# Recurrent mixer of a three-layer kernel: the products of w issued first at a scan, one scaled copy taken into a product, and a scale spread by transposes

## The chip, the cores and the metric

The kernel runs on one core of one Trainium2 chip. The metric is the device time of one execution in microseconds (us), from the first to the last instruction and a little around them; lower is better. The engines of a core are named as the profile names them: PE (TensorE's matmuls) and PEld (its weight loads), DVE (VectorE), ACT (ScalarE), POOL (GpSimd) and SP (SyncE, which issues most of the DMAs).

## What is computed

The whole kernel is a hybrid layer with three mixers and an MLP, an attention layer with an MLP, and a recurrent layer (RWKV-7) with an MLP, on 512 positions of width 1024, in 32-bit floats. The change lies in the recurrent mixer alone. Of its reference this matters:

```python
kk = heads(k * k_k)
kk = kk / jnp.maximum(jnp.sqrt(jnp.sum(kk * kk, axis=-1, keepdims=True)), 1e-12)
for d in range(2):
    ...
    decay = jnp.exp(-jnp.exp(w_log.astype(F32)))
    a = jax.nn.sigmoid(a0[d] + (xa @ a1[d]) @ a2[d])
    ...
    o = rwkv7_scan(*ins)

def step(state, inp):
    r_t, w_t, k_t, v_t, kk_t, a_t = inp
    sa = jnp.einsum('bhvk,bhk->bhv', state, -kk_t)
    state = (state * w_t[:, :, None, :] + sa[..., None] * (kk_t * a_t)[:, :, None, :]
             + v_t[..., None] * k_t[:, :, None, :])
    return state, jnp.einsum('bhvk,bhk->bhv', state, r_t)
```

There are 16 heads of 64, and two directions d; in the second the sequence runs backwards.

## The kernel before

The recurrence is not stepped through. `rwkv` puts two heads on the 128 partitions (a pair p, 0 to 7) and treats a pair in one direction as a stream q = 2p + d, 0 to 15. The 512 positions of a stream are 8 chunks of 64. Within a chunk everything is matrix products; from chunk to chunk a 64x64 state per head goes on. A stream passes three stages, written as generators, and a pair one more:

- `pair(p)` (L1278 to L1298): the keys of a pair are normalised. The squares are summed per head on PE (L1169), POOL takes the power -1/2 (L1172), DVE spreads the result over a 128x512 tile (L1176), and PE turns that tile over with four matmuls against the identity (L1179); DVE multiplies the keys by it (kk, L1292) and ACT makes a half of them (kkh, L1294).
- `prep(q)`: decays, gates and the scores. L1309 is the matmul of the decays and gates, L1311 to L1325 their functions on ACT, L1317 DVE's running sum along the positions, L1326 the product that reads kkh, L1335 and L1336 the products with the decays (ar and bk), L1350 the scores on PE and L1353 their masks on DVE. Two of the masked tiles (sc) go to DRAM through eight DMAs (lu, L1360).
- `invert(q)`: POOL inverts the 16x16 diagonal blocks of the scores (L1418, L1420, thirty small instructions), SP stores them (xu, L1427) and loads them in another layout (X, L1431); then DVE turns X over (L1439), and PE, DVE and ACT complete the inverse (L1446 to L1479).
- `scan(q)`: L1494 makes w and vs of all chunks on PE, taken to SBUF by ACT (L1495, L1497). Then products of all chunks: kb with vs (L1504, DVE scales it to n, L1505), w with kb (L1509, DVE adds the identity to make m, L1510), w with the scores (L1515, DVE adds it to ar, L1516), and the scores with vs (L1523, into the output's PSUM tile). Then the chain over the chunks: six times a PE product of m and n (L1528) and a DVE step (L1529) that makes the next n; PE adds each chunk's output (L1533). A norm and a gate follow (L1538 to L1565).

The loop at the end of `rwkv` steps a clock t; every 16 steps a new stream enters each stage, so that in one period a scan, the prep and the inversion of the next streams, and the big "fill" products (fil: L1214, L1230, L1247, 128x512 each) are interleaved on every engine. All instructions of an engine run in the order in which they were put in its queue; a scheduler sets that order from the order of the code, the yields and priorities. An instruction at the head of a queue that waits for another engine holds back all that stands behind it. A 32-bit matmul of the program is two MATMUL instructions in the trace; a transpose is one.

Of the kernel before, what the change touches and what calls it, by code (L numbers as in the profile page):

```python
# [8 lines left out]
F32 = mybir.dt.float32  # L9
F32R = mybir.dt.float32r  # L10
AF = mybir.ActivationFunctionType
ALU = mybir.AluOpType
# [5 lines left out]
S = 512  # L18
# [991 lines left out]
class L3:  # L1010
# [120 lines left out]
    def rwkv(self, lp, rkd, xr, vm, tw, ta, sg):  # L1131
        nc, tc, I = self.nc, self.tc, self.I
        with ExitStack() as cx:
            pool = lambda n, b, **kw: cx.enter_context(tc.tile_pool(name=n, bufs=b, **kw))
            arp, vsp, bkp, unp, sp, wk = (pool(n, b) for n, b in (
                ("ar", 4), ("vs", 3), ("bk", 1), ("un", 2), ("s3", 2), ("wk", 2)))
# [9 lines left out]
            eye = lp.tile([128, 64], F32, name="eye")  # L1146
# [12 lines left out]
            def c8(x):  # L1159
                return x.rearrange("p (c t) -> p c t", c=8)  # L1160

            def flip(x, d):
                return x[:, ::-1] if d else x

            def head_scale(sq, fn):

                ps = self.psm.tile([128, S], F32, tag="mm", name="mm")
                for b in range(4):
                    nc.tensor.matmul(ps[:, 2 * b:2 * b + 2], sq[:, b * 128:(b + 1) * 128], bones, start=True, stop=True)  # L1169
                c = sp.tile([128, 8], F32, tag="hs", name="hs", bufs=4)  # L1170
                fn(c, ps[:, 0:8])
                nc.gpsimd.tensor_tensor(c, c, self.mhalf, op=ALU.pow)  # L1172
                for _ in range(7):
                    yield
                e = T().rearrange("p (b h t) -> p b h t", b=4, h=2)
                nc.vector.tensor_copy(e, c.rearrange("p (b h) -> p b h", h=2).unsqueeze(3).to_broadcast([128, 4, 2, 64]))  # L1176
                ps = self.psm.tile([128, S], F32, tag="mm", name="mm")
                for b in range(4):
                    nc.tensor.matmul(ps[:, b * 128:(b + 1) * 128], e[:, b].rearrange("p h t -> p (h t)"), self.ident,  # L1179
                                     start=True, stop=True)  # L1180
                return ps

            turn = [0]
# [11 lines left out]
            def mm():  # L1195
                return self.psm.tile([128, 8, 64], F32, tag="mm", name="mm")

            H = [(h, slice(64 * h, 64 * h + 64), slice(64 - 64 * h, 128 - 64 * h)) for h in range(2)]
# [79 lines left out]
            def pair(p):  # L1278

                r[p], k[p] = (self.xnp.tile([128, S], F32, tag="xl", name=n) for n in "rk")  # L1280
                nc.sync.dma_start(k[p], rkd[p, 1])
                nc.sync.dma_start(r[p], rkd[p, 0])
                for _ in range(8):
                    yield
                wst = lora2(p, 0, 2)
                kkr, sq = T(), T()
                nc.scalar.activation(kkr, k[p], AF.Copy, scale=self.vec("k_k", p))
                nc.scalar.activation(sq, kkr, AF.Square)
                yield
                ps = yield from head_scale(sq, lambda c, ps: nc.vector.tensor_scalar_max(c, ps, 1e-24))  # L1290
                kk = wk.tile([128, S], F32, tag="kk", name="kk", bufs=1)
                nc.vector.tensor_tensor(kk, kkr, ps, op=ALU.mult)  # L1292
                kkh = wk.tile([128, S], F32, tag="kkh", name="kkh", bufs=1)
                nc.scalar.activation(kkh, kk, AF.Copy, scale=0.5)  # L1294
                rkw = wk.tile([128, 128], F32, tag="rkw", name="rkw")
                nc.vector.tensor_scalar_mul(rkw, bfull, self.vec("r_k", p))
                P[p] = wst, kk, kkh, rkw
                yield  # L1298

            def prep(q, C):  # L1300

                p, d = divmod(q, 2)
                wst, kk, kkh, rkw = P[p]

                ps, pa = (self.psm.tile([128, S], F32, tag="mm", name="mm") for _ in range(2))
                for i, (a, b) in enumerate(((0, 0), (0, 1), (1, 0))):
# [3 lines left out]
                s = T()  # L1310
# [12 lines left out]
                nc.scalar.copy(dl, dp[:, :, 64])  # L1323
                kd = T()
                nc.scalar.activation(kd, al, AF.Identity, bias=omka[:, p:p + 1], scale=hka[:, p:p + 1])  # L1325
                nc.vector.scalar_tensor_tensor(al, al, 1.0, flip(kkh, d), ALU.add, ALU.mult)  # L1326
                yield
                ar = C["ar"] = arp.tile([128, 2, S], F32, tag="ar", name="ar", bufs=3)
                ar0, ar1 = ar[:, 0], ar[:, 1]
# [3 lines left out]
                def pairs(h, c):  # L1333
                    return bk[64 * h:64 * h + 64, c, 1 - h:3 - h].rearrange("p a t -> p (a t)")
                nc.vector.tensor_tensor(c8(ar0), c8(flip(kk, d)), dp[:, :, 0:64], op=ALU.mult)  # L1335
                nc.vector.tensor_tensor(bk[:, :, 1, :], c8(al), c8(s), op=ALU.mult)  # L1336
                yield
                nc.vector.tensor_tensor(kd, flip(k[p], d), kd, op=ALU.mult)
                for h, rw, ow in H:
# [142 lines left out]
            def scan(q, C):  # L1482
# [3 lines left out]
                vs, sc, X, ar, dl, kb, za = (C[n] for n in ("vs", "sc", "x", "ar", "dl", "kb", "za"))  # L1486
                ar1 = ar[:, 1]
                w = self.hp.tile([128, 8, 64], F32, tag="h", name="w")
                for g in range(2):
                    gs = slice(4 * g, 4 * g + 4)  # L1490
                    ps = self.psm.tile([128, 4, 128], F32, tag="mm", name="mm")
                    for c in range(4):
                        for h, rw, ow in H:
                            nc.tensor.matmul(ps[rw, c, :], X[rw, 4 * g + c, :], za[rw, 4 * g + c, :], start=True, stop=True)  # L1494
                    nc.scalar.activation(w[:, gs], ps[:, :, 64:128], AF.Copy, scale=-1.0)  # L1495
                    for h, rw, ow in H:
                        nc.scalar.activation(vs[rw, gs, h, :], ps[rw, :, 0:64], AF.Copy, scale=-1.0)  # L1497
                yield
                m = self.hp.tile([128, 8, 64], F32, tag="h", name="m")
                n = self.hp.tile([128, 8, 64], F32, tag="h", name="n")  # L1500
                ps = mm()
                for c in range(7):
                    for h, rw, ow in H:
                        nc.tensor.matmul(ps[rw, c, :], kb[:, h, c, :], vs[:, c, h, :], start=True, stop=True)  # L1504
                nc.vector.tensor_tensor(n[:, 0:7], ps[:, 0:7], dl[:, 0:7].unsqueeze(2).to_broadcast([128, 7, 64]), op=ALU.mult)  # L1505
                ps = mm()
                for c in range(1, 7):
                    for h, rw, ow in H:
                        nc.tensor.matmul(ps[rw, c, :], w[rw, c, :], kb[rw, h, c, :], start=True, stop=True)  # L1509
                nc.vector.tensor_tensor(m[:, 1:7], ps[:, 1:7], eye.unsqueeze(1).to_broadcast([128, 6, 64]), op=ALU.add)  # L1510
                yield
                ps = mm()
                for c in range(1, 8):
                    for h, rw, ow in H:
                        nc.tensor.matmul(ps[rw, c, :], w[rw, c, :], sc[h][rw, c, 64:128], start=True, stop=True)  # L1515
                nc.vector.tensor_tensor(c8(ar1)[:, 1:8], c8(ar1)[:, 1:8], ps[:, 1:8], op=ALU.add)  # L1516
                po = pop.tile([128, 8, 64], F32, tag="o3", name="o3")
                pc = scp.tile([128, 8, 64], F32, tag="sc3", name="sc3")

# [1 line left out]
                for c in range(8):  # L1521
                    for h, rw, ow in H:
                        nc.tensor.matmul(po[rw, c], sc[h][:, c, 64:128], vs[:, c, h, :], start=(c == 0), stop=False,  # L1523
                                         skip_group_check=True)
                yield
                for c in range(1, 7):
                    for h, rw, ow in H:
# [235 lines left out]
```

## Time and profile before

| what | value |
|---|---|
| median of 3 runs | 2976.93 us (2967.24 to 2978.59) |
| the profiled execution's own time | 2985.52 us |
| its span | 2983.7 us |
| PE busy | 2838.5 us, 95% |
| PEld busy | 2269.1 us, 76% |
| DVE busy | 1632.7 us, 55% |
| ACT busy | 1286.8 us, 43% |
| POOL busy | 221.2 us, 7% |
| mean granted TensorE clock | 0.982 of full speed |
| PE's share of the chain that ended last | 75% |

Busy time is the union of an engine's instructions. The chain that ended last is followed back from the last instruction, at each step to what released it. In rows of a timeline the first number is the start in us from the start of the span, the second the duration in us, and what stands in brackets is how long the engine stood idle before and what ended that. Matmuls are pipelined, so that the durations of neighbours overlap; what a run of matmuls takes is read from the start of the first to the start of what follows it.

### The profile page before, as it was taken

What the parts mean: (1) busy time and instruction counts of PE and PEld (TensorE: products, weight loads), DVE (VectorE), ACT (ScalarE), POOL (GpSimd) and SP (SyncE); (2) the same over time, 40 slices, a digit from 0 to 9 for tenths busy, and PEclk for the clock granted to TensorE, in tenths of its full rate; (3) what the DMA queues carried; (4) which work ended last, traced back from release to release, by engine and by line L of the source; (5) the groups of instructions that cost most, each with busy time, mean ns of one, the idle gap of its engine ahead of it and who ended that gap; (6) DMA issues with size and microseconds to landing.
All of it is one profiled execution on the core that took longest, in us unless ns stands there. A gap on an engine that the chain in (4) does not pass through costs nothing.

```text
span 2983.7 us, 53131 instructions
## 1 busy us (share of the span) xinstructions
PE 2838.5 (95%) x21704; PEld 2269.1 (76%) x21704; DVE 1632.7 (55%) x3381; ACT 1286.8 (43%) x2458; POOL 221.2 (7%) x628
## 2 busy tenths in 40 slices
PE   7999999999999999999999999888999998699998
PEld 6877778777898888877798889745666666488887
DVE  5566684645462334666663335773556656743445
ACT  6565662565352223355553223453444443333222
POOL 0000000000000000000000000002343332100000
PEclk9999999999999999999999999999999999799999
DMA  4211123223323223122222223212212111312231
GB/s 138 90 42 61 36 75 107 88 92 118 101 80 95 92 95 124 41 89 73 61 85 92 99 92 127 90 63 64 51 33 51 31 35 16 120 61 95 93 113 36
DMA packets 140452, 234.73 MB, mean 79 GB/s; under 512 B 63088, under 2 KB 85360, under 8 KB 140080
## 3 DMA queue, kind: packets, MB, share of 16 engines
q1 hardware_dynamic: 137888, 229.40, 24.4%
q8 instruction: 171, 2.80, 0.4%
q10 hardware_dynamic: 2320, 1.93, 0.2%
q14 instruction: 73, 0.60, 0.1%
HBM read 220.72 MB, written 10.55 MB: 78 GB/s over the span
## 4 chain that ended last, share of the span: by engine, by line
PE 75%; DVE 8%; POOL 4%; DMA 4%; issue 4%; ACT 3%; SPq 2%; DVEq 0%; POOLq 0%; ACTq 0%
PE mm L80 57%; PE mm L1090 2%; PE o L732 2%; POOL tmp L1418 2%; PE mm L416 2%; POOL x L1420 1%; SPq L1431 1%; PE tr L722 1%; PE o L950 1%; PE mm L761 1%; DMA xu<-x 1%; PE tr L924 1%; DVE sqa L265 1%; PE mm L903 1%; DMA lt<-lu 1%
## 5 line engine op out<-in xcount | busy, mean ns | idle before, releaser
L80 PE MATMUL mm<-xh,wh 128*128 128x512 f32 (+1 forms) x2072 | 738.7, 358 | 10.4 <-ACT xh L69 6.3
L80 PE MATMUL mm<-xl,wh 128*128 128x512 f32 (+1 forms) x2072 | 736.7, 357 | 0.3 <-DVE xl L70 0.3
L80 PE MATMUL mm<-xh,wl 128*128 128x512 f32 (+1 forms) x2072 | 731.8, 355 | 2.1 <-DVE wl L65 2.1
L63 ACT CAST wh<-wr 128x1024 fp32r<-128x1024 f32 (+1 forms) x335 | 348.7, 1044 | 752.9 <-PE mm L80 609.4
L65 DVE TENSOR_TENSOR wl<-wr,wh 128x1024 fp32r<-128x1024 f32 (+1 forms) x335 | 406.9, 1216 | 460.2 <-ACT wh L63 450.2
L80 PEld LDWEIGHTS mm<-xh,wh 128*128 128x128 f32 x2072 | 392.1, 190 | 73.9 <-ACT xh L69 7.3
L80 PEld LDWEIGHTS mm<-xh,wl 128*128 128x128 f32 x2072 | 391.8, 189 | 60.4 <-issue 3.5
L80 PEld LDWEIGHTS mm<-xl,wh 128*128 128x128 f32 x2072 | 392.1, 190 | 56.2 <-issue 3.3
L80 PE MATMUL mm<-hl,wh 128*128 128x512 f32 (+1 forms) x880 | 306.0, 348 | 0.0
L80 PE MATMUL mm<-hh,wl 128*128 128x512 f32 (+1 forms) x880 | 304.5, 347 | 0.0
L80 PE MATMUL mm<-hh,wh 128*128 128x512 f32 (+1 forms) x880 | 304.5, 347 | 0.0
L80 PEld LDWEIGHTS mm<-hl,wh 128*128 128x128 f32 x880 | 167.2, 190 | 22.8 <-DVE hl L70 0.5
L80 PEld LDWEIGHTS mm<-hh,wl 128*128 128x128 f32 x880 | 167.1, 190 | 22.1
L80 PEld LDWEIGHTS mm<-hh,wh 128*128 128x128 f32 x880 | 166.9, 190 | 22.1
L241 DVE TENSOR_TENSOR acc<-acc,mm 128x256 f32<-128x256 f32 (+1 forms) x88 | 47.4, 541 | 179.3 <-PE mm L80 179.3
L275 POOL TENSOR_TENSOR r<-r,mhalf 128x2 f32<-128x2 f32 x24 | 23.3, 970 | 1256.6 <-DVE r L274 1256.6
L265 DVE TENSOR_TENSOR sqa<-sqa,sq 128x256 f32<-128x256 f32 x182 | 75.3, 422 | 54.8 <-ACT sq L264 50.5
L69 ACT CAST hh<-t 128x512 fp32r<-128x512 f32 (+1 forms) x106 | 57.0, 539 | 77.5 <-DVE t L212 68.4
L674 DVE CUSTOM_DVE_ANT_0 s<-mm,cmask 128x128 f32<-128x128 f32 (+3 forms) x128 | 59.8, 487 | 46.9 <-PE mm L756 23.1
L70 DVE TENSOR_TENSOR hl<-t,hh 128x512 fp32r<-128x512 f32 (+1 forms) x106 | 62.2, 589 | 35.3 <-ACT hh L69 34.8
L1377 ACT COPY vs<-mm 64x256 f32<-64x256 f32 x64 | 23.5, 367 | 131.7 <-PE mm L1372 130.8
L676 ACT ACTIVATE s<-s,m 128x128 f32<-128x128 f32 (+3 forms) x128 | 71.1, 557 | 13.4 <-DVE m L674 12.1
(413 smaller groups left out, 4786.9 us busy)
## 6 DMA issues: line engine op xcount, KB each, us to landing
wr<-in_mlp_w_dram SPq DMA_DIRECT2D x128, 512.0 KB, 3.5
wr<-in_w_ffn_in_dram SPq DMA_DIRECT2D x44, 512.0 KB, 3.5
wr<-in_w_mg_dram SPq DMA_DIRECT2D x24, 512.0 KB, 3.6
wr<-in_w_br_dram SPq DMA_DIRECT2D x24, 512.0 KB, 3.5
wr<-in_attn_w_in_dram SPq DMA_DIRECT2D x18, 512.0 KB, 3.5
wr<-in_w_ffn_out_dram SPq DMA_DIRECT2D x16, 512.0 KB, 3.5
wr<-in_w_kv_dram SPq DMA_DIRECT2D x12, 512.0 KB, 4.0
wr<-in_nsa_w_dram SPq DMA_DIRECT2D x8, 512.0 KB, 4.1
```

Source lines behind the costliest of these rows:

```text
L63: nc.scalar.copy(hi, raw)
L65: nc.vector.tensor_tensor(lo, raw, hi.bitcast(F32), op=ALU.subtract)
L69: self.nc.scalar.copy(hi, src)
L70: self.nc.vector.tensor_tensor(lo, src, hi.bitcast(F32), op=ALU.subtract)
L80: nc.tensor.matmul(ps, l, r[:, s0:s1], start=(n == 0), stop=(n == 3 * nk - 1))
L265: nc.vector.tensor_tensor(self.acc, self.acc, t, op=ALU.add)
L416: nc.tensor.matmul(ps[:, b % 2, :], l[:, t], r, start=(n == 0), stop=(n == 23))
L674: nc.vector.tensor_tensor_reduce(s, ps, mask, -1.0, 3e38, ADD, ALU.min, m)
L676: nc.scalar.activation(s, s, AF.Exp, bias=m, scale=-1.0, accum_out=d)
L732: nc.tensor.matmul(po[hh * 64:hh * 64 + 64, c + x0:c + x1], vv[w][:, b, vo:vo + 64], pts[hh][w][:, b, x0:x1], start=(w + i == 0), stop=Fal ...
L1090: nc.tensor.matmul(ps, ws[m][:, i * 128:(i + 1) * 128], xk[i][:, s0:s1], start=(i == 0), stop=(i == NT - 1))
L1418: nc.gpsimd.tensor_tensor(t, x[:, :m, i:i + 1].to_broadcast([128, m, n]), lt[:, i:i + 1, i + 1:].to_broadcast([128, m, n]), op=ALU.mult)
```

## The change

Four edits, all in `rwkv`:

1. In `head_scale` the four matmuls against the identity become four `transpose` instructions.
2. kkh is no longer made. L1326 multiplies by kk instead, and the half goes into L1336, which becomes a `scalar_tensor_tensor` with a factor 0.5.
3. In `scan` the code issues the two copies of w ahead of the four of vs.
4. In `scan` the products of w (with kb, then with the scores) are issued ahead of that of kb with vs, and ar's addition is issued after the product of the scores with vs.

```diff
@@ head_scale
-                    nc.tensor.matmul(ps[:, b * 128:(b + 1) * 128], e[:, b].rearrange("p h t -> p (h t)"), self.ident,
-                                     start=True, stop=True)
+                    nc.tensor.transpose(ps[:, b * 128:(b + 1) * 128], e[:, b].rearrange("p h t -> p (h t)"), self.ident)
@@ pair
-                kkh = wk.tile([128, S], F32, tag="kkh", name="kkh", bufs=1)
-                nc.scalar.activation(kkh, kk, AF.Copy, scale=0.5)
@@ prep
-                nc.vector.scalar_tensor_tensor(al, al, 1.0, flip(kkh, d), ALU.add, ALU.mult)
+                nc.vector.scalar_tensor_tensor(al, al, 1.0, flip(kk, d), ALU.add, ALU.mult)
...
-                nc.vector.tensor_tensor(bk[:, :, 1, :], c8(al), c8(s), op=ALU.mult)
+                nc.vector.scalar_tensor_tensor(bk[:, :, 1, :], c8(al), 0.5, c8(s), ALU.mult, ALU.mult)
@@ scan
+                pz = []
                 for g in range(2):
...
                     nc.scalar.activation(w[:, gs], ps[:, :, 64:128], AF.Copy, scale=-1.0)
+                    pz.append((gs, ps))
+                for gs, ps in pz:
                     for h, rw, ow in H:
                         nc.scalar.activation(vs[rw, gs, h, :], ps[rw, :, 0:64], AF.Copy, scale=-1.0)
                 yield
...
+                ps = mm()
+                for c in range(1, 7):
+                    for h, rw, ow in H:
+                        nc.tensor.matmul(ps[rw, c, :], w[rw, c, :], kb[rw, h, c, :], start=True, stop=True)
+                nc.vector.tensor_tensor(m[:, 1:7], ps[:, 1:7], eye.unsqueeze(1).to_broadcast([128, 6, 64]), op=ALU.add)
+                pa = mm()
+                for c in range(1, 8):
+                    for h, rw, ow in H:
+                        nc.tensor.matmul(pa[rw, c, :], w[rw, c, :], sc[h][rw, c, 64:128], start=True, stop=True)
+                yield
                 ps = mm()
                 for c in range(7):
                     for h, rw, ow in H:
                         nc.tensor.matmul(ps[rw, c, :], kb[:, h, c, :], vs[:, c, h, :], start=True, stop=True)
                 nc.vector.tensor_tensor(n[:, 0:7], ps[:, 0:7], dl[:, 0:7].unsqueeze(2).to_broadcast([128, 7, 64]), op=ALU.mult)
...
                         nc.tensor.matmul(po[rw, c], sc[h][:, c, 64:128], vs[:, c, h, :], start=(c == 0), stop=False,
                                          skip_group_check=True)
+                nc.vector.tensor_tensor(c8(ar1)[:, 1:8], c8(ar1)[:, 1:8], pa[:, 1:8], op=ALU.add)
                 yield
```

The lines taken out of `scan` are the same three products and the addition to ar in their old places. On the engines the order moves at these places. The numbers of lines differ by a few between the two programs.

PE, scan of stream 5, from the end of the products of all chunks on (o is the output's tile, sc the chain's, fil the fills): before

```order
L1523 MATMUL o_20883<-vs,wl 64x64
L1528 MATMUL sc_20884<-n,m 64x64 x2
L1247 MATMUL fil<-ys,wr 128x512
L1533 MATMUL o_20883<-n,ar 64x64 x2
L1230 MATMUL fil<-vm,wr 128x512
L1528 MATMUL sc_20884<-n,m 64x64 x2
```

and now

```order
L1522 MATMUL o_20874<-vs,wl 64x64
L1246 MATMUL fil<-ys,wr 128x512
L1528 MATMUL sc_20875<-n,m 64x64 x2
L1533 MATMUL o_20874<-n,ar 64x64 x2
L1229 MATMUL fil<-vm,wr 128x512
L1528 MATMUL sc_20875<-n,m 64x64 x2
```

One fill product stands ahead of the chain's first product instead of behind it; ahead of these rows the three products of all chunks stand as w with kb, w with the scores, kb with vs.

DVE, same stream (m, n and ar of the scan; t, kkh, kk and bk of the prep of the next stream; the second row is the running sum): before

```order
L1505 TENSOR_TENSOR n<-mm,dl 128x448
L1317 SCALAR_TENSOR_TENSOR t_20820<-const_17530,t_20820 128x512
L1510 TENSOR_TENSOR m<-mm,eye 128x384
L1326 SCALAR_TENSOR_TENSOR t<-t,kkh 128x512
L1516 TENSOR_TENSOR ar<-ar,mm 128x448
L1335 TENSOR_TENSOR ar<-kk,dp 128x512
L1336 TENSOR_TENSOR bk<-t,t_20820 128x8x64
L1529 SCALAR_TENSOR_TENSOR n<-sc_20884,dl,n 128x64
```

and now

```order
L1505 TENSOR_TENSOR m<-mm,eye 128x384
L1314 SCALAR_TENSOR_TENSOR t_20812<-const_17530,t_20812 128x512
L1524 TENSOR_TENSOR ar<-ar,mm 128x448
L1323 SCALAR_TENSOR_TENSOR t<-t,kk 128x512
L1515 TENSOR_TENSOR n<-mm,dl 128x448
L1332 TENSOR_TENSOR ar<-kk,dp 128x512
L1333 SCALAR_TENSOR_TENSOR bk<-t,t_20812 128x8x64
L1529 SCALAR_TENSOR_TENSOR n<-sc_20875,dl,n 128x64
```

m has gone from behind the running sum to ahead of it, and n from ahead of it to the third place behind it.

ACT, same stream, the copies of edit 3: before

```order
L1495 ACTIVATE w<-mm 128x256
L1497 ACTIVATE vs<-mm 64x4x64 x2
L1495 ACTIVATE w<-mm 128x256
L1497 ACTIVATE vs<-mm 64x4x64 x2
L69 CAST w_20956<-w_20953 128x256
```

and now

```order
L1493 ACTIVATE w<-mm 128x256
L1497 ACTIVATE vs<-mm 64x4x64 x2
L1493 ACTIVATE w<-mm 128x256
L1497 ACTIVATE vs<-mm 64x4x64 x2
L69 CAST w_20948<-w_20945 128x256
```

The scheduler has kept the order: nothing moved here.

## Rows read from the trace of the kernel before

**Rows 1.** Busy time by stretch: start:end, PE (count), PEld, DVE, ACT, POOL, granted clock, DMA.

```profile
2000.00:2064.00 64.00, 62.20 (x509) 34.34 (x511) 22.41 (x40) 23.27 (x45) 8.98 (x32) 1.00 0.31 87
2064.00:2550.00 486.00, 444.61 (x8567) 318.89 (x8560) 291.47 (x585) 200.30 (x461) 167.06 (x499) 0.96 0.17 36
```

**Rows 2.** PE's waits from 2060 to 2550: line, awaited; us in total, times, longest.

```profile
PE sc L1528 <- DVE n L1529: 18.4, 12, 8.1
PE sc L1528 <- DVE m L1510: 6.7, 14, 0.7
```

**Rows 3.** DVE's waits from 2060 to 2550, the one for a DMA.

```profile
DVE t L1439 <- DMA X<-xu: 22.4, 9, 7.8
```

**Rows 4.** DVE's timeline, from one stream's last mask to its X's turn.

```profile
2248.10 0.68 DVE L1353 TENSOR_TENSOR wl<-mm,const 128x512 f32<-128x512 f32 x1
...
2277.64 0.71 DVE L1439 STREAM_TRANSPOSE t<-X 128x512 f32<-128x512 f32 x1 [1.78 <-DMA X<-xu]
```

**Rows 5.** PE's timeline at L1179, once at the full clock.

```profile
2259.71 1.16 PE L1179 MATMUL mm<-ident,t 128*128 128x128 f32 x8
2260.80 1.15 PE L1551 MATMUL mm<-ident,t 64*64 64x64 f32 x32
2261.88 0.50 PE L1276 MATMUL mm<-sg1h,w 128*128 128x512 f32 x1
```

**Rows 6.** PE's timeline at four transposes of another stage, and what follows.

```profile
102.21 0.66 PE L857 MATMUL tr<-ident,vt 128*128 128x128 f32 x4 [0.32 <-ACT vt L667]
102.62 0.47 PE L80 MATMUL mm<-xl,wh 128*128 128x512 f32 x1
```

**Rows 7.** PE's timeline, scan of stream 5, from the last product of all chunks.

```profile
2238.05 0.22 PE L1523 MATMUL o<-vs,wl 128*64 128x64 f32 x1
2239.01 0.33 PE L1528 MATMUL sc<-n,m 64*64 64x64 f32 x4 [0.73 <-DVE m L1510]
2239.27 1.13 PE L1247 MATMUL fil<-ys,wr 128*128 128x512 f32 x2
2240.32 0.33 PE L1533 MATMUL o<-n,ar 64*64 64x64 f32 x4
...
2241.64 0.33 PE L1528 MATMUL sc<-n,m 64*64 64x64 f32 x4
```

**Rows 8.** DVE's timeline at the same place.

```profile
2237.28 1.22 DVE L1317 TENSOR_TENSOR_SCAN t<-const,t 128x512 f32<-128x512 f32 x1 [0.94 <-ACT t L1316]
2238.42 0.53 DVE L1510 TENSOR_TENSOR m<-mm,eye 128x384 f32<-128x384 f32 x1
2238.87 0.68 DVE L1326 SCALAR_TENSOR_TENSOR t<-t,kkh 128x512 f32<-128x512 f32 x1
2239.47 0.61 DVE L1516 TENSOR_TENSOR ar<-ar,mm 128x448 f32<-128x448 f32 x1
2240.00 0.68 DVE L1335 TENSOR_TENSOR ar<-kk,dp 128x512 f32<-128x512 f32 x1
2240.60 0.68 DVE L1336 TENSOR_TENSOR bk<-t,t 128x512 f32<-128x512 f32 x1
2241.20 0.27 DVE L1529 SCALAR_TENSOR_TENSOR n<-sc,dl,n 128x64 f32<-128x64 f32 x1
```

**Rows 9.** The instructions that write or read kkh: duration ns min/median/max, first and last start.

```profile
L1294 ACT ACTIVATE kkh<-kk x8: 629/630/632, 2002.2 to 2455.4; 128x512 f32<-128x512 f32 x8
```

**Rows 10.** Busy time of L1401 alone (PE, PEld), granted clock, DMA; the transposes of bk.

```profile
2253.00:2256.00 3.00, 1.01 (x16) 0.87 (x16) 1.00 0.02 6
```

**Rows 11.** Busy time by stretch, as rows 1: a half-speed stretch.

```profile
2134.90:2138.30 3.40, 3.40 (x41) 3.15 (x36) 1.52 (x3) 0.54 (x1) 2.58 (x11) 0.50 0.02 5
```

**Rows 12.** PE's timeline around that half-speed stretch.

```profile
2132.62 0.18 PE L1466 MATMUL mm<-t,wh 32*32 32x32 f32 x1 [1.31 <-DVE t L1459]
...
2134.93 2.07 PE L1179 MATMUL mm<-ident,t 128*128 128x128 f32 x8
...
2138.61 0.50 PE L1276 MATMUL mm<-sg1h,w 128*128 128x512 f32 x1
```

More of the change, by code (lines that the diff above doesn't have):

```diff
@@ L1292, in pair @@
                 nc.vector.tensor_tensor(kk, kkr, ps, op=ALU.mult)
-                kkh = wk.tile([128, S], F32, tag="kkh", name="kkh", bufs=1)
-                nc.scalar.activation(kkh, kk, AF.Copy, scale=0.5)
                 rkw = wk.tile([128, 128], F32, tag="rkw", name="rkw")
                 nc.vector.tensor_scalar_mul(rkw, bfull, self.vec("r_k", p))
-                P[p] = wst, kk, kkh, rkw
+                P[p] = wst, kk, rkw
                 yield
@@ L1302, in prep @@
                 p, d = divmod(q, 2)
-                wst, kk, kkh, rkw = P[p]
+                wst, kk, rkw = P[p]
                 ps, pa = (self.psm.tile([128, S], F32, tag="mm", name="mm") for _ in range(2))
@@ L1505, in scan @@
                 nc.vector.tensor_tensor(n[:, 0:7], ps[:, 0:7], dl[:, 0:7].unsqueeze(2).to_broadcast([128, 7, 64]), op=ALU.mult)
[L1506 to L1516, printed above, removed]
                 po = pop.tile([128, 8, 64], F32, tag="o3", name="o3")
```

## The prediction, made before the changed kernel ran

> **What bounds the kernel now.** I began with busy time by stretch [rows 1]. The change lies in the recurrent mixer. While its streams begin, from 2000 to 2064, PE is busy for 62.20 of 64 us; in the steady part, from 2064 to 2550, for 444.61 of 486 us, so that 41 us of idle PE are left, in sixteen periods of about 30 us each. PE is the bound there, but not alone. PE's waits [rows 2] name the rest: the chain's product L1528 waits for the DVE step before it (18.4 us, 12 times), and its first product waits for m (6.7 us, 14 times). The first of these two has its cause elsewhere: DVE's own waits [rows 3] show that L1439, which turns X over, waits for the DMA that brings X, 22.4 us in 9 of the 16 streams, and a chain step stands behind it in DVE's queue. X has a long way: masks on DVE, a store, a load, thirty POOL instructions, a store and a load. In one period it takes from 2248.10 to 2277.64, 29.5 us, nearly all of it [rows 4]. Two loops thus run side by side at almost the same pace: PE's queue, and the way of X. **Where X is the later one, time saved on PE between the masks and L1439 only makes the wait for X longer.**
>
> The other way round, where L1439 finds X there, PE's and DVE's queues decide. These are 7 streams of 16, one of them the first, which has no scan ahead of it.
>
> **The change part by part.**
>
> *Transposes for four matmuls.* At the full clock the eight instructions of L1179 take from 2259.71 to 2260.80, 1.09 us [rows 5]. A transpose is one instruction instead of two; four of another stage take 102.62 - 102.21 = 0.41 us [rows 6]. I take 0.44 for the place here, so 0.65 us less for each pair, 5.2 us over eight pairs. The lower bound is nothing (the transposes cost what the pairs of matmuls did), the upper 5.2. Behind L1179 stand L1551 and L1276 with no idle time in rows 5, so the saving moves on to the next scan. Whether it reaches the end depends on X: a pair's L1179 lies between an odd stream's masks and its L1439, the very stretch in which X is under way. By the position of the 9 waits [rows 3] it is swallowed for five of the seven later pairs and passes for two; that of pair 0, ahead of everything where PE is full [rows 1], passes as well. That makes 3 x 0.65 = **1.95 us gained**.
>
> *The products of w first.* On PE itself nothing is gained: the same three products stand one behind the other. What counts is when the chain's first product L1528 can start, and when its second can. Before, it waits for m, which stands behind the running sum on DVE: the sum starts at 2237.28, m at 2238.42, L1528 at 2239.01, after 0.73 us of idle PE [rows 7, 8]. Now m is early, and n is late: behind the running sum stand ar, t and then n. The running sum still waits for ACT, whose order has not changed. With the distances of rows 8 from start to start (sum 1.14, ar 0.53, t 0.60) n starts at 2237.28 + 1.14 + 0.53 + 0.60 = 2239.55 and, at the 0.61 us of ar, which has the same shape, ends at 2240.16. With the 0.06 us from m's end (2238.95) to L1528 (2239.01), the first product starts at 2240.22. Ahead of it PE now does one fill of 1.05 us (2239.27 to 2240.32, rows 7), from 2238.27, where L1523 ends, to 2239.32, and then stands idle for 0.90 us instead of 0.73. From there to the second product PE has 0.26 us for the first product (2239.01 to 2239.27) and 1.32 us for L1533 and the other fill (2240.32 to 2241.64), so the second product comes at 2240.22 + 1.58 = 2241.80 instead of 2241.64. Its n, from the first L1529, is there by then: DVE reaches that at 2239.55 + 0.53 + 0.60 + 0.60 = 2241.28 and ends at 2241.55. **So the chain comes 0.16 us later, not earlier**: a wait for m is exchanged for a slightly longer wait for n, since DVE has the same work between the running sum and the first step of the chain either way. In the streams with a wait for X the delay vanishes in it; in six others it passes, 6 x 0.16 = **1.0 us lost**. The bounds: if the second product were held back by all of n's delay, 2240.16 - 2238.95 = 1.21 us, 14 times, 16.9 us lost; if the wait for m went without a successor, 6.7 us gained [rows 2]. I take 0.16, since every term of it stands in rows of this very place.
>
> *The half of the keys.* L1294 took 0.63 us on ACT, eight times [rows 9]. Nothing that the trace shows waits for it, and its reader L1326 comes a scan later: nothing gained, however small PE's load. Its cover is ACT's idle time in that place; ACT is busy for 200.30 of 486 us [rows 1]. L1336 becomes a scalar_tensor_tensor of the same 128x512; L1326, which is one already, and L1336 have 0.68 us each in rows 8: no change. If the kind cost a tenth more, it would be 0.07 us, 16 times, 1.1 us at most.
>
> *The queues.* POOL's and SP's orders are the same but at one place: in the first streams two loads of k and r (and one of weights) now come before X's loads on SP instead of behind them. X's loads wait for the store of xu there, which covers the issues of k and r; their bytes may delay X a little. I take nothing, and one us for the range, since this is the longest of the waits for X.
>
> The sum is 1.0 - 1.95 = -0.95 us. On the profiled execution of 2985.52 us this gives 2984.6; the median of the runs lies 8.6 us below that execution, at 2976.93, and the forecast for it is **2976.0 us**, no change. A measurement here tells about 0.5%, 14.9 us, from no change; the three runs alone differ by 11.35 us.
>
> **The rivals.**
>
> *The waits go, and are not replaced (faster).* If n came before PE reaches the chain, and all eight savings of L1179 passed, 6.7 + 5.2 = 11.9 us would be gained: 2965.0. For it speaks that DVE stands idle for 0.94 us ahead of the running sum in rows 8, where n would fit. Against it: n's place in the queue is behind the sum, and X [rows 3] would swallow most. [...]
>
> [...]
>
> *n holds the chain (slower).* The mechanism is DVE's queue: n stands behind the running sum, which waits for ACT. It costs little only because a fill covers PE until 2239.32 and because DVE reaches the first L1529 no sooner than 2241.28. If the fill ahead of L1528 is itself held up (its PSUM tile is freed late by an ACT copy that stands behind the same ACT work), PE meets the wait bare. It decides from the point at which the first L1528 starts later than about 2240.9, 0.7 us after my 2240.22: then L1529 waits for PE too. The price is up to 16.9 us, worked out above; without a gain beside it that is 2976.9 + 16.9 = 2994. For it speaks that the wait is there in every steady period; against it, 0.7 us of room.
>
> *The change does nothing at the end.* All savings fall into waits for X: 2976.9 + 1.0 = 2978. It can't be told from the forecast and shares its chance.
>
> **How the numbers follow.** The forecast, with the case that all is swallowed, has 0.72. The faster rival has 0.14, of which 0.12 beyond 0.5% (other savings of the same sign included); the clock 0.06, of which 0.01 beyond; n 0.08, all counted as beyond 2991.8, the bound of 0.5%. So faster 0.12, same 0.79, slower 0.09. The range goes from 2962, the full gain with two clock stretches, to 2990, the clock rival and 2 us for the rest; 0.12 and about 0.08 are left out. No more than half of it comes from the terms of the sum; the rest is the clock and the way of X, which differ from run to run.
>
> **What would show it.** In the changed profile L1179 has 32 instructions instead of 64, and about 0.45 us from its first to what follows. PE's wait of L1528 for m is gone, and in its place stands a wait for n's first product by DVE, of some 0.5 to 0.9 us in about 14 streams. DVE's waits for X stay near 22 us or grow by one or two; kkh is gone and ACT is 5.0 us less busy. The steady part stays within 3 us of 486. The prediction is wrong if the wait for n is absent, if the periods without a wait for X shrink by half a microsecond or more, or if n's wait is above 1.5 us.

## The result, and the profile after

The changed kernel takes 2998.28 us (median of 6 runs, 2989.33 to 3005.61) against 2978.70 (6 runs) of the kernel before on the same chip: a ratio of 1.0068, 95% interval 1.0055 to 1.0082. It is slower by more than 0.5%, and the forecast of 2976.0 (2962 to 2990) was wrong. The profiled execution has a span of 2993.2 us and a mean granted clock of 0.979.

The loss is where the streams run. From the first copy of w (ACT L1495 before, L1493 after) of stream 0 to that of stream 15 it takes 2547.8 - 2068.7 = 479.1 us before and 2556.3 - 2062.5 = 493.8 after, 14.7 more. At its beginning the changed kernel was 6.2 us ahead, and behind it the two need 436.0 and 437.0.

Busy time by stretch, as [rows 1]: in the same 486 us PE is busy for 15 us less, and the clock is lower.

```profile
2064.00:2550.00 486.00, 429.61 (x8305) 308.54 (x8304) 284.98 (x573) 188.69 (x439) 162.45 (x482) 0.94 0.16 34
```

DVE's and PE's waits from 2060 to 2560, as [rows 3, 2]. The wait for m is gone and one for n (L1515) stands in its place, as forecast; but the waits for the chain step L1529 and for X have grown as well, from 18.4 to 29.3 and from 22.4 to 32.0.

```profile
DVE t L1436 <- DMA X<-xu: 32.0, 10, 8.0
PE sc L1528 <- DVE n L1529: 29.3, 13, 8.2
PE sc L1528 <- DVE n L1515: 11.3, 14, 1.1
```

PE's timeline at the transposes, as [rows 5]: 0.59 us from the first to what follows instead of 1.09.

```profile
2258.75 0.66 PE L1179 MATMUL mm<-ident,t 128*128 128x128 f32 x4
2259.34 1.15 PE L1551 MATMUL mm<-ident,t 64*64 64x64 f32 x32
```

PE's and then DVE's timeline at the chain of the scan of stream 5, as [rows 7, 8]: the order is that of the prediction, and the times nearly.

```profile
2228.07 0.22 PE L1522 MATMUL o<-vs,wl 128*64 128x64 f32 x1
2228.23 1.13 PE L1246 MATMUL fil<-ys,wr 128*128 128x512 f32 x2
2230.45 0.33 PE L1528 MATMUL sc<-n,m 64*64 64x64 f32 x4 [1.09 <-DVE n L1515]
...
2231.88 0.33 PE L1528 MATMUL sc<-n,m 64*64 64x64 f32 x4
```

```profile
2227.47 1.23 DVE L1314 TENSOR_TENSOR_SCAN t<-const,t 128x512 f32<-128x512 f32 x1 [0.97 <-ACT t L1313]
2228.61 0.59 DVE L1524 TENSOR_TENSOR ar<-ar,mm 128x448 f32<-128x448 f32 x1
...
2229.78 0.61 DVE L1515 TENSOR_TENSOR n<-mm,dl 128x448 f32<-128x448 f32 x1
...
2231.52 0.27 DVE L1529 SCALAR_TENSOR_TENSOR n<-sc,dl,n 128x64 f32<-128x64 f32 x1
```

So each part did what it was said to do, and yet the stage is longer. What is new is a beat of two: before, the periods of the streams 2 to 14 (from copy to copy of w) take 29 to 32 us, and one 35; after, from stream 3 on, they take 36 to 39 and 29 us in turn. One such pair, by the timelines of DVE, PE and POOL around the scan of stream 5:

```profile
2240.50 0.71 DVE L1436 STREAM_TRANSPOSE t<-X 128x512 f32<-128x512 f32 x1 [5.00 <-DMA X<-xu]
```

```profile
2242.68 0.48 PE L1528 MATMUL sc<-n,m 64*64 64x64 f32 x4 [5.28 <-DVE n L1529]
```

```profile
2241.50:2251.70 10.20, 9.03 (x94) 7.41 (x98) 3.75 (x10) 2.05 (x5) 1.65 (x1) 0.50 0.13 26
```

```profile
2254.84 1.64 POOL L1542 TENSOR_TENSOR rs<-rs,mhalf 128x8 f32<-128x8 f32 x1 [6.25 <-DVE rs L1541]
2256.44 0.21 POOL L1415 TENSOR_TENSOR tmp<-x,lt 128x15 f32<-128x15 f32 x1
```

The X of stream 6 comes late, and DVE waits 5.00 us for it; a chain step stands behind, and PE waits 5.28 for that. Then the granted clock is 0.50 for 10.2 us, by a windows row. The norm of that scan therefore comes late too, and POOL, which takes its power (L1542), begins the inversion of stream 7 right behind it, without a pause, 8.4 us after that stream's first lt load (SP, 2248.04). Before, it is some 4 us in the odd streams. From 2064 to 2560 the half-speed stretches sum to 58.0 us after and 37.5 before. L1179 and L1551 take 2138.61 - 2134.93 = 3.68 us where the clock is 0.50 [rows 11, 12] and 2261.88 - 2259.71 = 2.17 at the full clock [rows 5]; by these two the difference of 20.5 us accounts for some 20.5 x (1 - 2.17 / 3.68) = 8.4 of the 14.7 us, an estimate. The rest is waits. What makes X late in the even streams is seen on SP, where lu is issued. SP's timeline for stream 6, after and then before (x4 is four DMAs in a row):

```profile
2209.20 2.84 SPq L1357 DMA_DIRECT2D lu<-wh  x4
2212.14 1.80 SPq L1357 DMA_DIRECT2D lu<-wl  x4
2216.89 1.13 SPq L1408 DMA_DIRECT2D lt<-lu  x2
```

```profile
2217.32 1.72 SPq L1360 DMA_DIRECT2D lu<-wh  x4
2219.14 1.80 SPq L1360 DMA_DIRECT2D lu<-wl  x4
2222.15 1.13 SPq L1411 DMA_DIRECT2D lt<-lu  x2
```

The first four stores take 1.1 us longer to issue, and lt, which waits for them to land, follows 2.95 us after the last issue instead of 1.21. The DMA view of the 1.0 us from 2209.5 on (queue, kind: packets, MB, share of 16 engines; then the DMAs issued and their median time to landing) names a second user; before, in 2 us from 2217 on, there is none:

```profile
q1 hardware_dynamic: 135, 0.01, 7.5%
q8 instruction: 1, 0.02, 5.9%
issues: line engine op xcount, KB each, median us to landing
lu<-wh SPq DMA_DIRECT2D x2, 8.0 KB, 2.6
```

```profile
q1 hardware_dynamic: 288, 0.02, 8.0%
issues: line engine op xcount, KB each, median us to landing
lu<-wh SPq DMA_DIRECT2D x4, 8.0 KB, 1.5
```

Nothing in the trace names the engine that these packets belong to, 171 of 16,384 bytes each, which begin from 31.4 to 2974.6 us; their distances point to PE. From one packet to the next PE starts 252.5 instructions (matmuls and weight loads) in the median, between 207 and 300 in eight of ten cases; DVE starts 12, between 5 and 44. By the page PE has 2 x 21672, 253 for each packet. The first row is the page before, the others the page after:

```profile
PE 2838.5 (95%) x21704; PEld 2269.1 (76%) x21704; DVE 1632.7 (55%) x3381; ACT 1286.8 (43%) x2458; POOL 221.2 (7%) x628
PE 2832.7 (95%) x21672; PEld 2264.8 (76%) x21672; DVE 1632.7 (55%) x3381; ACT 1280.8 (43%) x2450; POOL 222.0 (7%) x628
...
q8 instruction: 171, 2.80, 0.4%
```

The packets are read here as PE's program, loaded in parts as it runs. **A transpose is two PE instructions (weight load and matmul) fewer than a 32-bit matmul; each pair loses eight, 64 in all by the two pages, and the later packets move against the program.** In the streams 4, 6, 8, 10, 12 and 14 the packets with the numbers 98, 107, 116, 124, 134 and 143 begin 1.83 to 6.88 us ahead of the last mask before, and from 0.20 us ahead of it to 0.03 behind it after. That became the theory once the first eight experiments had left only few others. The even streams can be met one after the other since the place of the packets nearly repeats with each pair: in both kernels there are, from pair 1 on, 2212 to 2348 instructions of PE and nine packets from one pair's L1179 to the next, and nine times 253 is 2277.

### The profile page after: what moved, and what is told of

It is laid out like the page before. It is cut to its first block, busy times and chain, and to the rows that moved or that the text cites. A ratio compares the mean times of both kernels' runs of the same rounds, so it can differ in the third digit from the quotient of the medians.

```text
span 2993.2 us, 53093 instructions
## 1 busy us (share of the span) xinstructions
PE 2832.7 (95%) x21672; PEld 2264.8 (76%) x21672; DVE 1632.7 (55%) x3381; ACT 1280.8 (43%) x2450; POOL 222.0 (7%) x628
## 4 chain that ended last, share of the span: by engine, by line
PE 75%; DVE 8%; DMA 4%; POOL 4%; issue 4%; ACT 3%; SPq 2%; DVEq 0%; POOLq 0%; ACTq 0%
PE mm L80 57%; POOL tmp L1415 2%; PE o L732 2%; POOL x L1417 2%; PE mm L416 1%; PE mm L1090 1%; PE tr L722 1%; SPq L1428 1%; PE o L950 1%; DMA xu<-x 1%; PE mm L761 1%; DMA lu<-wl 1%; DMA lt<-lu 1%; PE tr L924 1%; PE mm L903 1%
## 5 line engine op out<-in xcount | busy, mean ns | idle before, releaser
L80 PE MATMUL mm<-xh,wh 128*128 128x512 f32 (+1 forms) x2072 | 739.4, 358 | 10.2 <-ACT xh L69 6.3
L1528 PEld LDWEIGHTS sc<-n,m 64*64 64x64 f32 x384 | 19.5, 138 | 93.0 <-DVE n L1529 49.3
```

Of the source, the lines that this page charges most:

```text
L80: nc.tensor.matmul(ps, l, r[:, s0:s1], start=(n == 0), stop=(n == 3 * nk - 1))
```

## The experiments

"lu stalled" in the table counts the streams 2 to 15 in which lu's eight issues end more than 3.3 us after the last mask, in even and odd streams (seven of each); "landing late" those in which lt is issued over 2 us after that. Both come from SP's and DVE's timelines of the profiled run. The kernel before has medians of 2976.7 to 2979.4 beside these runs.

| run | median us | ratio to before (95%) | lu stalled, even / odd | landing late, even / odd |
|---|---|---|---|---|
| before | 2978.70 | | 1 / 0 | 0 / 6 |
| the change | 2998.28 | 1.0055 to 1.0082 | 7 / 0 | 5 / 1 |
| transposes_alone | 2993.36 | 1.0023 to 1.0069 | 7 / 0 | 2 / 0 |
| half_alone | 2979.88 | 0.9990 to 1.0017 | 1 / 0 | 0 / 7 |
| order_alone | 2976.18 | 0.9986 to 1.0005 | 1 / 1 | 0 / 6 |
| transposes_half | 2997.39 | 1.0040 to 1.0083 | 7 / 0 | 4 / 2 |
| pair1_only | 2976.69 | 0.9976 to 1.0000 | 1 / 0 | 0 / 5 |
| all_but_pair1 | 2998.56 | 1.0045 to 1.0084 | 7 / 0 | 3 / 2 |
| single_pass | 2993.26 | 1.0034 to 1.0062 | 7 / 0 | 2 / 2 |
| transposes_twice | 2979.94 | 0.9993 to 1.0021 | 1 / 0 | 0 / 6 |
| after_plus16 | 2985.30 | 1.0016 to 1.0041 | 1 / 0 | 0 / 6 |
| after_plus32 | 2983.14 | 1.0003 to 1.0029 | 0 / 0 | 0 / 7 |
| transposes_filled | 2978.50 | 0.9989 to 1.0018 | 0 / 0 | 0 / 6 |
| before_plus16 | 2980.50 | 0.9992 to 1.0013 | 0 / 1 | 2 / 4 |
| before_plus80 | 2983.10 | 1.0002 to 1.0027 | 0 / 7 | 4 / 2 |
| after_filled | 2984.51 | 0.9998 to 1.0026 | 0 / 0 | 0 / 7 |
| no_transposes | 2981.62 | 0.9989 to 1.0017 | 1 / 1 | 0 / 6 |
| lu_late_even | 2998.14 | 1.0038 to 1.0080 | made late | 6 / 2 |

In these 17 runs without lu_late_even there are 272 streams (all sixteen of each run). In 72 of them an instruction packet begins between 0.75 us before and 2.65 us after the last mask: there lu's issues end 3.55 to 4.55 us after it, 4.07 on average. In the other 200 they end after 3.04 to 3.3 us, 3.07 on average, but for two. (The bounds of this stretch were chosen by these same streams.) Of the 272 landings 120 are late, 2.85 us on average from lu's last issue to lt's first, against 1.24 for the others; each late one has a packet that begins between 0.4 us before and 1.3 us after lu's last issue, and none of the others has one from 0.4 us before to 0.75 us after it.

**Which edit it is.** Edit 1 alone, 2 alone, 3 and 4 together, 1 and 2 together, each as its hunk of the diff above.

```diff
-                    nc.tensor.matmul(ps[:, b * 128:(b + 1) * 128], e[:, b].rearrange("p h t -> p (h t)"), self.ident,
-                                     start=True, stop=True)
+                    nc.tensor.transpose(ps[:, b * 128:(b + 1) * 128], e[:, b].rearrange("p h t -> p (h t)"), self.ident)
```

> The kernel before with the four transposes in head_scale and nothing else. Theory O (the order of the products at a scan made the kernel slower): no change beyond 6 us of the kernel before (about 2979), since the order of the products is the old one. Theory T (the transposes did it: they save PE 0.6 us a pair, which turns into longer waits for X, and the clock answers): 2990 to 3000. The instructions of L1179 number 32, and take about 0.45 us a pair instead of 1.09.

> The kernel before without kkh, the half taken into L1336, nothing else. PE's order is the old one to the last row. Theories O and T: no change, within 6 us of 2979. If it is slower by 10 us or more, DVE's scalar_tensor_tensor into the strided bk, or ACT's missing copy, matters and both theories miss something.

> The kernel before with edits 3 and 4 (the products of w first, the copies of w first in the code) and the old matmuls and kkh. Theory O: slower, 2993 to 3003, with DVE's waits for X above 28 us, POOL starting the inversion of odd streams behind the norm of the scan before, and PE half-speed stretches behind waits of 3 us in odd scans. Theory T: within 6 us of 2979.

> The change without its order of products (edits 1 and 2). Theory O: within 6 us of 2979, perhaps 2 us faster. Theory T: 2990 to 3000. If both this and the order alone are slower by a part of the 20 us, any shift between PE and the way of X costs, and neither edit is the cause by itself.

The two with transposes lose 15.9 and 19.9 us, the two without nothing. The theory that the order of the products did it falls. In its profiled run transposes_alone was quick (a span of 2979.3) though its lu stalls in all seven even streams: so the stall alone does not fix the loss, which differs from run to run (2978.58 to 3008.22). In the six profiled runs with a late lu in the even streams the span mostly grows with the even streams that also land late: 2 of them in transposes_alone (2979.3) and single_pass (2984.7), 3 in all_but_pair1 (2993.0), 4 in transposes_half (2997.6), 5 in the change (2993.2), 6 in lu_late_even (2999.3). These are single profiles, and no run was made for it, so this is a lead and not shown; late landings without a stall are not enough, since before_plus80 has four in the even streams and a span of 2977.1.

**Order of the queues, time saved, or the transposes' mode.** The transposes also move a few instructions in the first streams, all of it because of pair 1. In the first two kernels the transposes are taken for some pairs only:

```diff
+                    if tr:            # tr is an argument, set for pair 1 alone; all_but_pair1: for the seven others
+                        nc.tensor.transpose(ps[:, b * 128:(b + 1) * 128], e[:, b].rearrange("p h t -> p (h t)"), self.ident)
+                        continue
                     nc.tensor.matmul(ps[:, b * 128:(b + 1) * 128], e[:, b].rearrange("p h t -> p (h t)"), self.ident,
```

> The transposes stand in pair 1 alone, where they change the order of the queues in the first streams (on SP the loads of k, r and of weights go ahead of X's loads; on PE one fill moves); the seven other pairs keep the matmuls. Three theories of the loss with the transposes alone (2993.4 against 2977.5 us). Theory Q: the order of the queues in the first streams sets a phase that stays; then this kernel has the whole loss, 2990 to 2998 us, and the lu issues of even streams take 3.7 us or more instead of 3.05. Theory S: the time saved on PE at each pair turns into longer waits and a lower clock; then one pair of eight gives at most 2 us, 2977 to 2980. Theory M: the transposes themselves let the clock fall, at each pair; then likewise 2977 to 2980.

> The transposes stand in all pairs but pair 1, and every queue has the order of the kernel before. Theory Q (order of the queues in the first streams): no loss, 2972 to 2980 us, and lu issues of 3.05 us in even streams. Theory S (time saved on PE) and theory M (the transposes' mode and the clock): seven eighths of the loss, 2988 to 2995 us, with the alternating periods of the changed kernel.

The third takes matmuls of one instruction, the fourth each transpose twice:

```diff
+        self.identr = self.const.tile([128, 128], F32R, name="identr")
+        nc.vector.tensor_copy(self.identr, self.ident)
...
-                e = T().rearrange("p (b h t) -> p b h t", b=4, h=2)
+                e = T().bitcast(F32R).rearrange("p (b h t) -> p b h t", b=4, h=2)
...
-                    nc.tensor.matmul(ps[...], e[:, b]..., self.ident, start=True, stop=True)
+                    nc.tensor.matmul(ps[...], e[:, b]..., self.identr, start=True, stop=True)
```

```diff
-                    nc.tensor.matmul(ps[...], e[:, b]..., self.ident, start=True, stop=True)
+                    for _ in range(2):
+                        nc.tensor.transpose(ps[:, b * 128:(b + 1) * 128], e[:, b].rearrange("p h t -> p (h t)"), self.ident)
```

> No transposes: the four 32-bit matmuls against the identity become four matmuls of the type fp32r, one instruction each, so that PE saves about what the transposes save; all queues have the order of before. The scale is rounded to that type. Theory S: loss of the transposes, 2988 to 2996 us. Theories Q and M: 2972 to 2980 us.

> Each of the four transposes is issued twice into the same place: eight transposes for eight instructions of matmuls, so that PE saves about 0.3 us a pair at most (eight transposes at 0.10 us against 1.09 us). SP's, DVE's and ACT's queues have the order of before but for one load of weights, which stands two places earlier on SP. Theory M: the loss, 2988 to 2998 us, and more half-speed stretches. Theories Q and S: 2973 to 2981 us.

The order of the queues falls (pair1_only has it and loses nothing; all_but_pair1 lacks it and loses 20.4 us). So does the mode: sixty-four transposes cost nothing, thirty-two matmuls of the other type cost 15.1 us. What is left has two names here, since PE's time and its number of instructions fall together. SP's timelines for stream 6 in all_but_pair1 and then in pair1_only show the stall again, and its absence:

```profile
2215.98 2.70 SPq L1363 DMA_DIRECT2D lu<-wh  x4
2218.78 1.81 SPq L1363 DMA_DIRECT2D lu<-wl  x4
```

```profile
2217.14 1.72 SPq L1363 DMA_DIRECT2D lu<-wh  x4
2218.96 1.79 SPq L1363 DMA_DIRECT2D lu<-wl  x4
```

**Time saved or instructions moved.** Four or eight (and later twenty) matmuls that nobody reads, at the program's very start:

```diff
         make_identity(nc, self.ident)
+        for _ in range(4):
+            ps = self.psm.tile([128, S], F32, tag="mm", name="mm")
+            for _ in range(1):        # 2 for 32, 5 for 80 instructions
+                nc.tensor.matmul(ps[:, 0:1], self.ident, self.ident[:, 0:1], start=True, stop=True)
```

> The changed kernel with four 32-bit matmuls of one column added at the program's start, where PE stands idle until 11.15 us; nobody reads them. They are sixteen more PE instructions (eight weight loads, eight matmuls), and every other instruction keeps its place in every queue. Theory I (instruction loads): the traces hold packets of kind instruction, 16384 bytes each, one for about 255 PE instructions; in 160 streams of ten profiled runs the eight issues of lu take 3.04 to 3.15 us when none begins within -0.3 to +2.6 us of the last mask, and 3.6 to 4.6 when one does; one that begins from 0.3 us before to 0.8 us behind lu's last issue makes its landing 2.1 to 3.5 us long instead of 1.1 to 1.4. The transposes took eight PE instructions out of each pair, so that these loads come later against the program and fall on lu in the even streams. Sixteen more instructions put them back: by the times of the changed kernel, shifted by sixteen instructions, none of fifteen streams has a load on lu's issue, instead of eight. Expected: 2965 to 2980 us, below the changed kernel by 15 us or more. Theory S (the time saved on PE becomes longer waits and a lower clock): the stage's work is the same, so no change, 2992 to 3002 us.

> As the run with sixteen instructions more, with eight matmuls of one column, thirty-two PE instructions. Theory I: by the same shift of the times, no stream has a load on lu's issue and two have one on its landing: 2965 to 2982 us. Theory S: 2992 to 3002 us.

> The control: the kernel before with the same four matmuls of one column at the start. Theory I: by the shift of its own times the streams with a load on lu's issue fall from two to none and those with one on its landing from seven to six, all of them odd: 2968 to 2979 us, the same or a little faster. Theory S: 2975 to 2981 us, the same. Were the added matmuls worth something by themselves (a warmer clock at the start), this kernel would gain the 15 us as well.

PE's timelines at the start and SP's for stream 6, in after_plus16: the added work lies in PE's idle time, and the stall, 2200 us later, is gone.

```profile
1.57 1.87 PE L50 MATMUL mm<-ident 128*128 128x1 f32 x8 [1.57 <-POOL ident masks.py:199]
11.91 0.98 PE L276 MATMUL mm<-ones,sqa 128*128 128x1 f32 x4 [8.47 <-DVE sqa L269]
```

```profile
2220.93 1.72 SPq L1361 DMA_DIRECT2D lu<-wh  x4
2222.76 1.80 SPq L1361 DMA_DIRECT2D lu<-wl  x4
```

With every instruction of the stage in its place, 13.0 and 15.1 us come back; the control gains nothing (2980.50, 1.5 us above what was expected of it by this theory). So the time saved is not the cause of these, and the position of the instruction loads is. Against the kernel before, 0.3% and 0.2% stay, and both medians lie above what was expected. Landings are late in six and seven odd streams, where two in all had been expected of the second run; but the kernel before has them in six odd streams too, so they do not explain what stays, and its cause is not shown.

The next run was to keep the saved time and the old number of instructions, the one after it does so for the whole change:

```diff
+                for b in range(2):
+                    nc.tensor.matmul(ps[:, b * 128:b * 128 + 1], e[:, b].rearrange("p h t -> p (h t)"), self.ident[:, 0:1],
+                                     start=True, stop=True)
                 for b in range(4):
                     nc.tensor.transpose(...)
```

> The transposes alone, and at each pair two 32-bit matmuls of one column ahead of them (eight PE instructions that write what the first two transposes write over), so that PE issues as many instructions as in the kernel before, and still saves some 0.3 us or more at each pair. The queues have the order of the kernel with the transposes alone. Theory I: the loads stand against the program as before; 2970 to 2981 us. Theory S: at least half of the loss, 2985 to 2995 us.

> The whole change, and at each pair two 32-bit matmuls of one column ahead of the transposes, so that PE issues as many instructions as before. Theory I: the whole change is then neutral, 2970 to 2982 us. Theory S, and every theory in which edits 2 to 4 add to the loss: 2985 us or more.

The losses are gone, but the first of these proves less than it was meant to. PE's timeline shows 1.03 us from the filler to what follows, so that only 0.06 us of 1.09 is saved:

```profile
2249.33 0.61 PE L1179 MATMUL mm<-ident,t 128*128 128x1 f32 x4
2249.80 0.63 PE L1182 MATMUL mm<-ident,t 128*128 128x128 f32 x4
2250.36 1.15 PE L1553 MATMUL mm<-ident,t 64*64 64x64 f32 x32
```

after_filled lies 2.5 us above its expected range; its interval allows no change and up to 0.26% more.

**The phase alone, and the delay alone.** Eighty instructions as above in the kernel before; edits 2 to 4 alone; and two stores more, which make lu late in the even streams without a change on PE:

```diff
+                if q % 2 == 0:
+                    lx = self.dram.tile([64, 16, 16], F32, tag="lx", name="lx", bufs=2)
+                    for b in range(2):
+                        nc.sync.dma_start(lx[8 * b:8 * b + 8].rearrange("c s t -> s c t"),
+                                          sc[0][16 * b:16 * b + 16, :, 16 * b:16 * b + 16])
```

> The kernel before with twenty 32-bit matmuls of one column at the program's start, in PE's idle time there: eighty PE instructions more, all queues as before. By the shift of its own times, the streams with an instruction load on lu's issue stay at two and those with one on its landing go from seven to ten of fifteen, in rows of neighbouring streams. Theory I: slower by 3 us or more, 2981 to 2995. Theory S (time saved on PE): nothing is saved, 2975 to 2981.

> Edits 2 to 4 without the transposes; PE's number of instructions is that of before. Theory I: neutral, 2970 to 2981 us. Would edits 2 and 4 together lose what neither lost alone: above 2985 us.

> The kernel before; in the even streams two stores more, of the first two tiles of lu into a tensor that nobody reads, stand ahead of lu's eight on SP (0.95 us of issue by the distance of two issues in the trace); PE's, DVE's and ACT's queues are as before, on SP one load of weights moves behind the lt loads of an even stream. Theory I with the way of X as the reason: a lu that is 0.95 us late in the even streams costs what the instruction loads cost there, 2983 to 2998 us. If the way of X in the even streams has room, and the loss comes from something else that the instruction loads do: 2974 to 2981 us.

lu_late_even has the loss with no matmul changed, 2998.14 us from four runs against 2998.28 (that the two agree so closely is luck, with runs from 2992.02 to 3004.38), and the beat with it: POOL begins 6.5 to 8.4 us after the first lt load in streams 5, 7, 9 and 13. SP's timeline for stream 6:

```profile
2222.89 0.78 SPq L1360 DMA_DIRECT2D lx<-wh  x2
2223.71 1.86 SPq L1365 DMA_DIRECT2D lu<-wh  x4
2225.66 1.80 SPq L1365 DMA_DIRECT2D lu<-wl  x4
```

The extra stores also moved a load of weights on SP, and in six even streams a packet then falls on the landing as well ("landing late" in the table); these weren't taken apart. no_transposes is neutral (2981.62, 0.6 us above its expected range). In before_plus80 the phase alone costs 3.7 us; there the stall is in the odd streams. Why a late lu is cheap there and dear in the even ones isn't settled: the odd counterpart wasn't tried, since it changes PE's order.

**A shorter way.** Every second lu store issued by POOL, in both kernels:

```diff
-                        nc.sync.dma_start(lu[u0:u0 + 8].rearrange("c s t -> s c t"),
+                        (nc.sync, nc.gpsimd)[b % 2].dma_start(lu[u0:u0 + 8].rearrange("c s t -> s c t"),
```

> The kernel before; every second of lu's eight stores is issued by POOL instead of SP, so that the issues of lu on SP take some 1.4 us instead of 3.05, if POOL issues its four in that time. PE's and ACT's queues are as before. Way of X as the reason: up to 1.6 us less in each of sixteen streams, of which those that wait for X keep most; 2955 to 2972 us. If POOL is slow to issue and lu lands later, slower: 2985 to 3010. If the way of X has room: 2975 to 2981.

> The changed kernel with the same split of lu's stores. Way of X as the reason: the loss and more comes back, 2960 to 2982 us. If POOL is slow to issue: 2995 to 3020.

The kernel before has 2981.34 (0.9994 to 1.0023), the changed one 2975.22 (0.9982 to 1.0017): the change's loss is gone, but neither is below the kernel before, for which 2955 to 2972 had been expected. In the kernel before the mean way of X (last mask to X's turn, streams 1 to 15) falls only from 28.44 to 28.15 us: SP's share of lu from 3.18 to 1.27, while it took 1.0 more from X's store to the first of its loads (3.10 to 4.12). No run beat the kernel before.

## Why the prediction was wrong

**Transposes: the step that failed.** Its size on PE was nearly right (0.50 us a pair instead of 0.65). What failed is what it was worth: "time saved on PE ... only makes the wait for X longer", so that its bounds went from nothing to 5.2 us gained, with 1.95 taken. The runs put 15.9 us lost in its place. The step took the way of X as a length of its own, which PE's queue doesn't touch. But the instruction packets, PE's by the count, go by DMA as well (q8 beside q1 in the DMA view): with one on lu's store the way was 1.0 us longer at the issue (4.07 against 3.07 us on average) and, with one on the landing, 1.6 us there (2.85 against 1.24). Taking instructions out of PE's queue moved these loads from harmless places onto the even streams' stores. The step on **the queues** has the same hole: it compared the order on SP and POOL, and the order was innocent (pair1_only); it did not ask where in time the loads of PE's program fall. Two of the prediction's own signs fail with it: DVE's waits for X grow to 32.0 us instead of staying near 22 or growing by one or two, and the steady part is 14.7 us longer instead of within 3.

**Products of w.** Right. The first product waits 1.09 us (0.90 forecast), and the second comes 2231.88 - 2228.07 = 3.81 us after the start of the last L1522 instead of 2241.64 - 2238.05 = 3.59 [rows 7], 0.22 later (0.16 forecast). order_alone, 2976.18, can't be told from no change.

**The half of the keys.** Right: half_alone is the same, and ACT is 6.0 us less busy on the page (1286.8 to 1280.8).

**The rivals.** "n holds the chain" did not happen. No run shows the terms of the clock in the range, two half-speed stretches fewer at its lower end and the clock rival at its upper; what the runs showed in their place is 20.5 us more at half speed, part of the loss (some 8.4 us by the estimate above), but not from the transposes: of the eight half-speed stretches from 2064 to 2560 seven stand at a PE wait of 2.8 to 5.3 us, at all eight places of L1179 in the changed kernel, where four transposes stand among matmuls, the granted clock is 1.00, and transposes_twice, with 64 transposes, takes 2979.94 us. The chance of 0.09 for slower by over 0.5%, and the upper end of 2990, were too small since every term of them came from PE, DVE and the clock, and none from the DMA queue of instructions, whose row stood on the page.

## What to carry to other kernels

In this kernel the number of PE's instructions, the busiest engine's, was a timing parameter of a loop with a DMA hop on its critical way: an edit that took out 64 of them moved instruction packets onto that hop and cost 15.9 us, several times the 8 x 0.50 us that it saved on PE. So, where a loop has such a hop, read queue and kind in the DMA view of its window, as well as the order of the queues. And test an unexplained loss by a few dead instructions at a point where the engine is idle: here sixteen and thirty-two of them brought 13.0 and 15.1 us back with none of the stage's work changed. If the time moves so, the phase is the first suspect, and judging an edit needs more than one phase.

## What was not expected of the hardware

An instruction packet of 16,384 bytes, PE's by the count, on lu's issue goes with a longer issue on SP: in stream 6 four stores took 2.84 us instead of 1.72, and all 72 streams with a packet at that place show it (issues that end 3.55 us or more after the mask, instead of some 3.07). How a packet holds them up is not shown. When a half-speed stretch follows such a wait, and why an odd stream forgives what an even one doesn't, stays open.
